# A recurrent layer step on one core: branch sums and weight splits given to VectorE, more row tiles of the out projection begun early, one mask product in place of two

## The chip, the cores and the metric

The kernel runs on one core of a Trainium2 chip. The metric is the device time of one execution in microseconds. The engines are named as in the profile: PE (TensorE; PEld is its weight load), DVE (VectorE, `V` in the code), ACT (ScalarE, `S`), POOL (GpSimd, `G`), and SP, whose queue issues most of the loads. Each engine works through its own list of instructions in order. Waits between engines go by semaphores.

## The reference

One inference step of a decoder layer with three token mixers side by side, for 512 prompt tokens and 8 x 4 sample tokens:

```python
h = rmsnorm(x, L['norm_pre_mix'])
proj = jnp.einsum('bsd,dc->bsc', h, L['w_in'])
xa, ga, bq, bf, bi, bg, cblk, gts = _split(proj, IN_SPLIT)
yA, nconv, nlru = rglru_branch(xa, ga, conv0, lru0, pos, ...)      # branch 0, width 512
yB, nhg = hgrn2_branch(bq, bf, bi, bg, hg0, lb, ...)               # branch 1, width 512
yC, nrw, nsh = rwkv7_branch(cblk, sh0, rw0, ...)                   # branch 2, width 512
br = jnp.stack([yA, yB, yC], axis=2)
up = jnp.einsum('bsnw,nwd->bsnd', br, L['w_branch'])
gates = jax.nn.sigmoid(gts.reshape(B, S, N_BRANCH, D_MODEL))       # D_MODEL = 1024
mix = jnp.einsum('bsd,de->bse', jnp.sum(gates * up, axis=2), L['w_out'])
x = x + rmsnorm(mix, L['norm_post_mix'])
h = rmsnorm(x, L['norm_pre_ffn'])
ff = (jax.nn.silu(h @ L['w_ffn_gate']) * (h @ L['w_ffn_up'])) @ L['w_ffn_down']
x = x + rmsnorm(ff, L['norm_post_ffn'])
x = x + rmsnorm((p @ L['w_ple']) * jax.nn.sigmoid(x @ L['w_ple_gate']), L['norm_ple'])
```

The change touches the sum over the three branches of gate times product, the product with `w_out` behind it, and, inside `rwkv7_branch`, the state update of the sample tokens: `st = st * wt - sk * (kkt * at) + vt * kt` for each of 8 sequences.

## The kernel before, in words

The 544 tokens are the columns of every tile, features are on the 128 partitions, so a tensor of width 1024 is 8 row tiles of 128x544 (`KD = 8`). A product of one row tile goes in two halves of 272 columns. Each fp32 operand is split in two parts, `hi` (a copy rounded to the format of the matmuls) and `lo` (what is left), and a product is hi·hi + hi·lo + lo·hi: three matmuls for each 128x128 block and half of the columns. Activations are split once (`act_h`, `act_l`). Weights are streamed: SP loads a row tile's weight into one of three buffers `raw`, ACT copies it to `hi` (L325) and a second engine subtracts to get `lo` (L326), half a tile (128x512) at a time. Which engine subtracts is read from a list `split_eng` with an entry for the first and one for the second half; a weight of the branches has only one half. The list holds `[V, V]` at first, `[G, G]` from the end of the RWKV part to the end of branch 2 and the gates of branch 1, and then `[V, V]` again. Three pairs of `hi` and `lo` halves are in flight. The weights of the first seven row tiles of `w_out` are kept (`held_weights`); their splits carry the names `ar<-raw` (`hi`) and `ar<-raw,ar` (`lo`), always on VectorE.

A branch (`branch`, L1487 on) goes over eight row tiles. For each, `th` is the gate (its tanh), `ps` the product of the branch with its weight (24 matmuls into a `pa` tile of two buffers), L1505 makes (th + 1) * ps on VectorE, and L1507 adds that to the row of the mix on GpSimd; the first branch writes the mix directly. The order of the branches is 0, 2, 1. The gates of branches 0 and 2 were computed earlier and put in DRAM (`gates`), from where SP loads them (L1501, `th<-gates`) into a work tile with two buffers; those of branch 1 stay on the chip.

Beside branch 2 runs the second half of HGRN2 (`hgrn_half(1)`), with raised priority: a scan by levels in which VectorE steps (L1302, L1305, L1306), small products on PE (`pb` tiles, four buffers) and masked copies out of them (L1328, L1317) follow each other, up to a last step L1355.

Behind branch 1, L1564 (ACT) and L1565 (VectorE) make `act_h` and `act_l` from each row of the mix, and the out projection runs by `by_halves`: first the prompt's first 272 columns of all row tiles, then `between_mix`, then the second half of the kept ones. Its first `ahead_of` row tiles (2) do all input rows but the last, then the last row of each of them, then each result is emptied: L1597 (a copy by ACT out of the `pb` tile) and L448 (its square). Each further row tile goes in one piece. `x` is loaded again for the residual (L168).

The update of the RWKV state for the sample tokens (`rw_decode`) goes by two pairs of heads in each of two calls. For a pair it spreads a 64x64 operand over the 8 sequences and masks it, for each of the two heads of the pair into 512 of the 1024 columns of `vm` (L993), and two matmuls follow.

No order is written out by hand: the code issues instructions in the order of the program with priorities (`high_priority`), and a scheduler with a timeline of its own sets, when the kernel is built, the order of each engine's list and of SP's loads. A change of an engine can thus move instructions elsewhere.

Of the kernel before, what the change touches and what calls it, by code (L numbers as in the profile page):

```python
# [12 lines left out]
ALU = mybir.AluOpType  # L13
# [4 lines left out]
NB = 8  # L18
# [4 lines left out]
KD = DM // P  # L23
# [8 lines left out]
NKEEP = 7  # L32
# [26 lines left out]
def kernel(  # L59
# [164 lines left out]
    smask = const.tile([64, NB], F32, name="smask")  # L224
# [703 lines left out]
    def rw_decode(y):  # L928

        v4, O4 = y.l4(y.v), y.l4(y.O)  # L930
        for m in range(2):
# [57 lines left out]
            V.tensor_tensor(O4[:, 2 * m:2 * m + 2, 256:288], ps[:, 0:2 * ND].rearrange("p (l n) -> p l n", l=2),  # L989
                            xo[:, :, 1, :], ALU.add)  # L990
            for i, l in enumerate(ls):
                for hp in range(2):
                    V.tensor_tensor(vm[0:64, 512 * hp:512 * hp + 512].rearrange("p (b n) -> p b n", b=NB),  # L993
                                    VUd[:, 2 * i + hp, :].unsqueeze(1).to_broadcast([64, NB, 64]),
                                    smask.unsqueeze(2).to_broadcast([64, NB, 64]), ALU.mult)
                ps = pb()
                with together():
                    for hp in range(2):
                        mm(ps[par[hp], :], KBtd[:, i, 64 * hp:64 * hp + 64], vm[0:64, 512 * hp:512 * hp + 512])
                sv = S0v[:, i]  # L1000
                V.tensor_tensor(sv, ps.rearrange("p (b n) -> p b n", b=NB), sv, ALU.add)
                V.tensor_tensor(sv, sv, y.PC[:, l, 4:12].unsqueeze(2).to_broadcast([P, NB, 64]), ALU.mult)
                G.dma_start(rws_out[:, l], sv)
# [209 lines left out]
    def hgrn_qvg(g):  # L1213

        q, v, gg = (alloc([P, 2, T], True) for _ in range(3))

        def silu2(dst, ct):
            ps = w_in_proj(ct)
            th = work.tile([P, T], F32, tag="ht", name=nm("th"))
            S.activation(half(th), ps[:, :, 0:272], AF.Tanh, scale=0.5)  # L1220
            V.scalar_tensor_tensor(half(dst), half(th), 1.0, ps[:, :, 0:272], op0=ALU.add, op1=ALU.mult)

        for l in range(2):
            silu2(j2(q)[:, l, :], BQ + 2 * g + l)
        for l in range(2):
            ps = w_in_proj(BI + 2 * g + l)
            S.activation(half(j2(v)[:, l, :]), ps[:, :, 0:272], AF.Copy)
        for l in range(2):
            silu2(j2(gg)[:, l, :], BG + 2 * g + l)
        return q, v, gg  # L1230
# [259 lines left out]
    def branch(n, yh, yl):  # L1490
        first = not mix
        if first:
            mix.append(gates[n] if n in gates else Rows(KD))
        m = mix[0]
        for j in range(KD):
            if n in gates:
                th = gates[n](j)
            else:
                th = work.tile([P, T], F32, tag="ht", name=nm("th"))
                if n in far:  # L1500
                    nc.sync.dma_start(th, far[n][:, j, :])  # L1501
                else:
                    gate(n, j, th)
            ps = proj(w_br[KD * n + j], 4, (yh, yl))
            V.scalar_tensor_tensor(half(m(j) if first else th), half(th), 1.0, ps[:, :, 0:272], op0=ALU.add, op1=ALU.mult)  # L1505
            if not first:
                G.tensor_tensor(m(j), m(j), th, ALU.add)  # L1507
        if n in gates and not first:
            gates[n].drop()
        yh.drop()  # L1510
        yl.drop()
# [39 lines left out]
    with tc.high_priority(1000):  # L1551
        yB = [hgrn_half(0, *fk[0], *qvg[0])]
    qvg.append(hgrn_qvg(1))
    branch(2, *yC)
    early_gates(1)
    with tc.high_priority(1500):
        yB.append(hgrn_half(1, *fk[1], *qvg[1]))
# [72 lines left out]
            f()  # L1630
        norm_ffn(0)

    by_halves([(w_out[j], KD) for j in range(KD)], HS, act, NKEEP, out_evac, between_mix, V)
    mix_steps = after_mix(1) + [lambda: norm_ffn(1)]
    p_hl = layer_input()
    ple = Rows(4 * NPLE // 2)
# [313 lines left out]
```

## Time and profile before

| | |
|---|---|
| times of three runs | 1212.57, 1194.4, 1202.06 us (median 1202.06) |
| the profiled execution | 1201.44 us, span 1199.7 us, mean granted clock 0.985 |
| busy, of the span | PE 1155.8 us (96%), DVE 763.5 (64%), ACT 582.9 (49%), POOL 317.8 (26%) |
| costliest split group on DVE, L326 | 234 instructions, 175.1 us |
| the same on POOL, L326 | 39 instructions, 60.2 us |

A row of a table by stretches reads: from and to in us from the span's start, length, then the busy time (and the number of instructions) of PE, PEld, DVE, ACT and POOL, the granted clock of PE, the busy share of the DMA engines and GB/s. A row of a timeline reads: start, duration, engine, line, operation, output and inputs, tile size, number of instructions taken together, and in brackets the idle time of the engine before it with what ended it. A row of groups reads: line, engine, operation, output and inputs, shape, number, busy time in all, mean duration in ns, idle time before them and what ended it.

### The profile page before, as it was taken

How to read it: one execution, taken by the hardware profiler on the slowest of the kernel's cores; microseconds unless marked ns; L12 is line 12 of the kernel's file. 1: busy time of each engine (PE TensorE's matmuls, PEld its weight loads, DVE VectorE, ACT ScalarE, POOL GpSimd, SP SyncE). 2: the span in 40 equal slices, each digit the busy share in tenths (PEclk: the TensorE clock that was granted, in tenths of full speed). 3: DMA queues.
4: the chain of work that ended last, by engine and by line, in shares of the span. 5: the costliest groups of instructions: out<-in, count | busy, mean ns of one | idle time of the engine just before them, and what ended most of it. 6: DMA issues, size and time to landing. Idle time of an engine off the chain costs nothing.

```text
span 1199.7 us, 24284 instructions
## 1 busy us (share of the span) xinstructions
PE 1155.8 (96%) x10048; PEld 1098.7 (92%) x10048; DVE 763.5 (64%) x1240; ACT 582.9 (49%) x1033; POOL 317.8 (26%) x367
## 2 busy tenths in 40 slices
PE   7999999999999999999999999999999999999995
PEld 6889999899899789889899898999999999999995
DVE  6789864944534759678214658765874576475766
ACT  6776355544633434453242555444552354255763
POOL 7327034310200002435543215101330330121001
PEclk9999999999999999989999999999999999999998
DMA  5212312122252431134522503123322332334302
GB/s 178 79 54 89 91 56 78 50 74 90 63 177 63 152 98 54 53 92 134 181 62 80 185 22 104 36 71 106 99 82 84 89 103 74 96 116 134 89 19 75
DMA packets 37470, 108.91 MB, mean 91 GB/s; under 512 B 4464, under 2 KB 6544, under 8 KB 37360
## 3 DMA queue, kind: packets, MB, share of 16 engines
q1 hardware_dynamic: 33856, 95.69, 26.1%
q0 software_dynamic: 3504, 11.67, 2.8%
q8 instruction: 79, 1.29, 0.4%
q14 instruction: 31, 0.25, 0.1%
HBM read 96.98 MB, written 10.36 MB: 89 GB/s over the span
## 4 chain that ended last, share of the span: by engine, by line
PE 75%; DVE 13%; DMA 4%; issue 4%; ACT 3%; POOL 0%; SPq 0%; DVEq 0%; ACTq 0%; POOLq 0%
PE pa L129 47%; PE pb L129 20%; PE pb L127 4%; PE pa L127 3%; DVE lo L326 2%; DVE ar L1302 1%; ACT hi L325 1%; DMA raw<-in_w_out_dram 1%; DVE ar L326 1%; PE pb L133 1%; DMA raw<-in_w_dn_b_dram 1%; PE pn L129 1%; DVE ar L1305 1%; PE pl L129 1%; DMA th<-gates 1%
## 5 line engine op out<-in xcount | busy, mean ns | idle before, releaser
L325 ACT ACTIVATE hi<-raw 128x512 fp32r<-128x512 f32 (+1 forms) x273 | 166.1, 610 | 310.4 <-PE pa L129 251.0
L326 DVE TENSOR_TENSOR lo<-raw,hi 128x512 fp32r<-128x512 f32 (+1 forms) x234 | 175.1, 751 | 151.4 <-ACT hi L325 147.0
L129 PE MATMUL pa<-act_h,hi 128*128 128x272 f32 (+1 forms) x1136 | 250.4, 296 | 0.5 <-ACT ar L544 0.3
L129 PE MATMUL pa<-act_h,lo 128*128 128x272 f32 (+1 forms) x1136 | 248.4, 294 | 1.5 <-DVE lo L326 1.5
L129 PE MATMUL pa<-act_l,hi 128*128 128x272 f32 (+1 forms) x1136 | 249.4, 295 | 0.0
L129 PE MATMUL pa<-ar,hi 128*128 128x272 f32 x1312 | 234.3, 292 | 9.8 <-ACT ar L475 5.6
L129 PEld LDWEIGHTS pa<-ar,hi 128*128 128x128 f32 x1312 | 191.9, 189 | 16.7 <-issue 7.0
L129 PEld LDWEIGHTS pa<-act_h,hi 128*128 128x128 f32 x1136 | 185.3, 192 | 5.4 <-issue 2.6
L129 PEld LDWEIGHTS pa<-act_l,hi 128*128 128x128 f32 x1136 | 185.0, 192 | 5.5 <-issue 3.8
L129 PEld LDWEIGHTS pa<-act_h,lo 128*128 128x128 f32 x1136 | 184.9, 192 | 5.3 <-issue 2.1
L129 PE MATMUL pa<-ar,lo 128*128 128x272 f32 x656 | 142.5, 291 | 0.0
L129 PE MATMUL pb<-act_h,ar 128*128 128x272 f32 x608 | 118.0, 290 | 3.9 <-ACT ar L448 1.9
L129 PEld LDWEIGHTS pa<-ar,lo 128*128 128x128 f32 x656 | 105.0, 190 | 2.2 <-issue 1.8
L129 PEld LDWEIGHTS pb<-act_h,ar 128*128 128x128 f32 x608 | 95.9, 188 | 5.6 <-ACT ar L448 2.1
L129 PE MATMUL pb<-ar,ar 64*64 64x64 f32 (+10 forms) x1496 | 91.4, 237 | 2.8 <-DVE st L905 1.6
L326 POOL TENSOR_TENSOR lo<-raw,hi 128x512 fp32r<-128x512 f32 x39 | 60.2, 1550 | 116.6 <-ACT hi L325 116.6
L129 PE MATMUL pb<-act_l,ar 128*128 128x272 f32 x304 | 88.1, 291 | 0.9 <-DVE act_l L1612 0.5
L129 PEld LDWEIGHTS pb<-ar,ar 64*64 64x64 f32 (+5 forms) x1496 | 75.5, 143 | 11.8 <-issue 4.2
L1718 POOL TENSOR_TENSOR ar<-raw,raw 128x512 f32<-128x512 f32 x10 | 14.6, 1456 | 202.6 <-DMA raw<-in_w_up_dram 202.6
L129 PEld LDWEIGHTS pb<-act_l,ar 128*128 128x128 f32 x304 | 57.2, 189 | 2.1 <-DVE act_l L1612 0.9
L326 DVE TENSOR_TENSOR lo<-ar,hi 128x512 fp32r<-128x512 f32 x40 | 34.5, 862 | 23.1 <-ACT hi L325 22.9
L422 DVE TENSOR_TENSOR ar<-ar,ar 128x544 fp32r<-128x544 f32 (+4 forms) x43 | 34.9, 818 | 12.9 <-ACT ar L421 11.2
(401 smaller groups left out, 1946.5 us busy)
## 6 DMA issues: line engine op xcount, KB each, us to landing
raw<-in_w_in_dram SPq DMA_DIRECT2D x61, 512.0 KB, 3.6
raw<-in_w_gate_dram SPq DMA_DIRECT2D x22, 512.0 KB, 3.6
raw<-in_w_up_dram SPq DMA_DIRECT2D x22, 512.0 KB, 3.6
raw<-in_w_dn_a_dram SPq DMA_DIRECT2D x24, 384.0 KB, 3.0
raw<-in_w_br_dram SPq DMA_DIRECT2D x24, 256.0 KB, 2.7
ar<-in_x_dram SPq DMA_DIRECT2D x16, 272.0 KB, 5.2
gates<-th POOLq DMA_DIRECT2D x16, 272.0 KB, 2.4
th<-gates SPq DMA_DIRECT2D x16, 272.0 KB, 2.9
```

The source lines that it names most:

```text
L127: PE.matmul(out, lhsT=lhsT, rhs=rhs, start=start, stop=stop, skip_group_check=True)
L129: PE.matmul(out, lhsT=lhsT, rhs=rhs, start=start, stop=stop)
L133: PE.transpose(out, in_, ident)
L325: S.activation(hi, raw, AF.Copy)
L326: eng.tensor_tensor(lo, raw, hi.bitcast(F32), ALU.subtract)
L422: V.tensor_tensor(lo, src, hi.bitcast(F32), ALU.subtract)
L1302: V.tensor_tensor(dv, bv, bv[:, :, :, hB - 1:hB].to_broadcast([P, 2, n // B, B]), ALU.subtract)
L1305: V.tensor_tensor(dv[:, :, :, 0:hB], dv[:, :, :, 0:hB], kv[:, :, :, 0:hB], ALU.mult)
L1718: G.tensor_tensor(q[0], a11, a21, ALU.subtract)
```

## The change

Four edits. The two mask products of a pair of heads become one instruction over 1024 columns (8 in all become 4). The sum of a branch into the mix goes from GpSimd to VectorE (16 instructions, for branches 2 and 1). The list `split_eng` is `[V, V]` for branch 2, so that its eight `lo` splits go from GpSimd to VectorE, and `[G, G]` again behind it. The out projection does all input rows but the last for four row tiles instead of two. Behind the first edit the line numbers are lower by one, and from the third on higher by one (L1564 becomes L1565, L1597 becomes L1598).

```diff
--- before.py
+++ after.py
@@ -989,10 +989,9 @@
             V.tensor_tensor(O4[:, 2 * m:2 * m + 2, 256:288], ps[:, 0:2 * ND].rearrange("p (l n) -> p l n", l=2),
                             xo[:, :, 1, :], ALU.add)
             for i, l in enumerate(ls):
-                for hp in range(2):
-                    V.tensor_tensor(vm[0:64, 512 * hp:512 * hp + 512].rearrange("p (b n) -> p b n", b=NB),
-                                    VUd[:, 2 * i + hp, :].unsqueeze(1).to_broadcast([64, NB, 64]),
-                                    smask.unsqueeze(2).to_broadcast([64, NB, 64]), ALU.mult)
+                V.tensor_tensor(vm[0:64, 0:1024].rearrange("p (h b n) -> p h b n", h=2, b=NB),
+                                VUd[:, 2 * i:2 * i + 2, :].unsqueeze(2).to_broadcast([64, 2, NB, 64]),
+                                smask.unsqueeze(1).unsqueeze(3).to_broadcast([64, 2, NB, 64]), ALU.mult)
                 ps = pb()
                 with together():
                     for hp in range(2):
@@ -1504,7 +1503,7 @@
             ps = proj(w_br[KD * n + j], 4, (yh, yl))
             V.scalar_tensor_tensor(half(m(j) if first else th), half(th), 1.0, ps[:, :, 0:272], op0=ALU.add, op1=ALU.mult)
             if not first:
-                G.tensor_tensor(m(j), m(j), th, ALU.add)
+                V.tensor_tensor(m(j), m(j), th, ALU.add)
         if n in gates and not first:
             gates[n].drop()
         yh.drop()
@@ -1551,7 +1550,9 @@
     with tc.high_priority(1000):
         yB = [hgrn_half(0, *fk[0], *qvg[0])]
     qvg.append(hgrn_qvg(1))
+    split_eng[:] = [V, V]
     branch(2, *yC)
+    split_eng[:] = [G, G]
     early_gates(1)
     with tc.high_priority(1500):
         yB.append(hgrn_half(1, *fk[1], *qvg[1]))
@@ -1630,7 +1631,7 @@
             f()
         norm_ffn(0)
 
-    by_halves([(w_out[j], KD) for j in range(KD)], HS, act, NKEEP, out_evac, between_mix, V)
+    by_halves([(w_out[j], KD) for j in range(KD)], HS, act, NKEEP, out_evac, between_mix, V, ahead_of=4)
     mix_steps = after_mix(1) + [lambda: norm_ffn(1)]
     p_hl = layer_input()
     ple = Rows(4 * NPLE // 2)
```

The order of every engine is the same as before up to the first of the updates of the RWKV sample state, and again from the fifth row tile of the out projection on. Between them it differs at three places.

**Branch 2 beside the second HGRN half.** VectorE's list before, around the fifth level of the scan; `th` with its number is the gate of one row tile of branch 2, `pa` its product, and L1505 makes gate times product:

```order
L1505 SCALAR_TENSOR_TENSOR th_6181<-th_6181,pa_6183 128x544
L1305 TENSOR_TENSOR ar_7001<-ar_7001,ar_4392 128x2x8x32
L1306 TENSOR_TENSOR ar_7001<-ar_7001,ar_5810 128x2x8x32
L1505 SCALAR_TENSOR_TENSOR th_6216<-th_6216,pa_6218 128x544
L1328 COPY_PREDICATED ar_6982<-lmask,pb_7111 64x8x2x16 x2
L1302 TENSOR_TENSOR ar_7000<-ar_6951 128x2x512
L1317 COPY ar_6982<-pb_7135 32x8x32
L1305 TENSOR_TENSOR ar_7000<-ar_7000,ar_4392 128x2x4x64
L1306 TENSOR_TENSOR ar_7000<-ar_7000,ar_5810 128x2x4x64
L1505 SCALAR_TENSOR_TENSOR th_6251<-th_6251,pa_6253 128x544
```

VectorE's list after, in the same place (all lines but L326 are one lower or, for the sum, L1506; `ar_4527` is a row of the mix; `lo_6288<-raw_6285,hi_6287` is a weight's split):

```order
L1504 SCALAR_TENSOR_TENSOR th_6177<-th_6177,pa_6179 128x544
L1305 TENSOR_TENSOR ar_6996<-ar_6996,ar_5806 128x2x16x16
L326 TENSOR_TENSOR lo_6288<-raw_6285,hi_6287 128x512
L1304 TENSOR_TENSOR ar_6997<-ar_6997,ar_4392 128x2x8x32
L1305 TENSOR_TENSOR ar_6997<-ar_6997,ar_5806 128x2x8x32
L1506 TENSOR_TENSOR ar_4527<-ar_4527,th_6177 128x544
L1504 SCALAR_TENSOR_TENSOR th_6212<-th_6212,pa_6214 128x544
L326 TENSOR_TENSOR lo_6323<-raw_6320,hi_6322 128x512
L1506 TENSOR_TENSOR ar_4527<-ar_4527,th_6212 128x544
L1327 COPY_PREDICATED ar_6978<-lmask,pb_7107 64x8x2x16 x2
L1301 TENSOR_TENSOR ar_6996<-ar_6947 128x2x512
L1504 SCALAR_TENSOR_TENSOR th_6247<-th_6247,pa_6249 128x544
```

Splits and sums of branch 2 now stand between the steps of the scan, and the copy out of the fifth level's product (`pb_7111`, now `pb_7107`) comes after two splits and two sums that were not in the list.

PE's list before, around the matmuls of the fifth level (`pb_7111`), in branch 2:

```order
L129 MATMUL pa_6218<-ar_5432,hi_6221 128x272 x2
L129 MATMUL pa_6218<-ar_5434,hi_6221 128x272 x2
L129 MATMUL pa_6218<-ar_5432,lo_6222 128x272 x2
L129 MATMUL pb_7111<-ar_7000 64x32 x16
L129 MATMUL pa_6253<-ar_5431,hi_6256 128x272 x2
L129 MATMUL pa_6253<-ar_5433,hi_6256 128x272 x2
L129 MATMUL pa_6253<-ar_5431,lo_6257 128x272 x2
```

PE's list after (the same product is `pb_7107`; `pa_6249` is the row that was `pa_6253`):

```order
L129 MATMUL pa_6249<-ar_5428,hi_6252 128x272 x2
L129 MATMUL pa_6249<-ar_5430,hi_6252 128x272 x2
L129 MATMUL pa_6249<-ar_5428,lo_6253 128x272 x2
L129 MATMUL pa_6249<-ar_5428,hi_6252 128x272 x2
L129 MATMUL pb_7107<-ar_6996 64x32 x16
L129 MATMUL pb_7131<-ar_6997 32x32 x8
L129 MATMUL pa_6249<-ar_5430,hi_6252 128x272 x2
```

The fifth level stood right before a row of the branch (`pa_6253`), and now stands in that row's last third: 57 instead of 41 branch matmuls lie between the fourth level's product and it.

**The loads of branch 2's gates.** SP's list before; a `raw` of `in_w_in` is a weight of the gates of branch 1, `in_x` the reload of x:

```order
L1501 DMA th_6286<-gates_3522 128x544
L168 DMA ar_7590<-in_x_dram 128x544 x2
L168 DMA ar_7591<-in_x_dram 128x544
L1501 DMA th_6321<-gates_3522 128x544
L168 DMA ar_7591<-in_x_dram 128x544
L330 DMA raw_6466<-in_w_in_dram 128x1024
L168 DMA ar_7592<-in_x_dram 128x544 x2
L330 DMA raw_6526<-in_w_in_dram 128x1024
L1501 DMA th_6356<-gates_3522 128x544
```

SP's list after, from the same row's gate (`th_6286`, now `th_6282`) on:

```order
L1500 DMA th_6282<-gates_3522 128x544
L330 DMA raw_6462<-in_w_in_dram 128x1024
L1500 DMA th_6317<-gates_3522 128x544
L168 DMA ar_7586<-in_x_dram 128x544 x2
L330 DMA raw_6522<-in_w_in_dram 128x1024
L168 DMA ar_7587<-in_x_dram 128x544 x2
L1500 DMA th_6352<-gates_3522 128x544
```

The two weights have moved up by some places, and four loads of x stand between the fourth gate load and the sixth, where six stood.

**The begin of the out projection.** ACT's list before; L1564 makes a row of `act_h`, and L325 are the `hi` halves of the row tiles of `w_out`: `raw_7683` is the third, `raw_7718` the fourth and `raw_7754`, `raw_7789`, `raw_7825`, `raw_7858` the fifth to the eighth:

```order
L1564 ACTIVATE act_h<-ar_4529 128x544
L325 ACTIVATE ar_7681<-raw_7683 128x512 x2
L1564 ACTIVATE act_h<-ar_4529 128x544
L1564 ACTIVATE act_h<-ar_4530 128x544
L325 ACTIVATE ar_7752<-raw_7754 128x512 x2
L325 ACTIVATE ar_7787<-raw_7789 128x512 x2
L325 ACTIVATE ar_7716<-raw_7718 128x512 x2
L1564 ACTIVATE act_h<-ar_4530 128x544
L325 ACTIVATE ar_7823<-raw_7825 128x512 x2
L325 ACTIVATE hi_7860<-raw_7858 128x512
```

ACT's list after (L1565 makes `act_h`; `raw_7669` is the third, `raw_7699` the fourth, `raw_7750`, `raw_7785`, `raw_7821` and `raw_7854` the fifth to the eighth):

```order
L1565 ACTIVATE act_h<-ar_4529 128x544
L325 ACTIVATE ar_7667<-raw_7669 128x512 x2
L1565 ACTIVATE act_h<-ar_4529 128x544
L325 ACTIVATE ar_7748<-raw_7750 128x512 x2
L1565 ACTIVATE act_h<-ar_4530 128x544
L325 ACTIVATE ar_7783<-raw_7785 128x512 x2
L325 ACTIVATE ar_7697<-raw_7699 128x512 x2
L1565 ACTIVATE act_h<-ar_4530 128x544
L325 ACTIVATE ar_7819<-raw_7821 128x512 x2
L325 ACTIVATE hi_7856<-raw_7854 128x512
```

The fifth row tile's halves have moved ahead of a row of the mix, and only two pairs, not three, stand between ACT's last two rows of the mix.

PE's list after, at the last input row of the four row tiles (`pb_7615`, `pb_7645`, `pb_7675`, `pb_7705`) and the begin of the fifth (`pb_7756`):

```order
L129 MATMUL pb_7615<-act_l,ar_7607 128x272
L129 MATMUL pb_7615<-act_h,ar_7608 128x272
L129 MATMUL pb_7645<-act_l,ar_7637 128x272
L129 MATMUL pb_7645<-act_h,ar_7638 128x272
L129 MATMUL pb_7675<-act_l,ar_7667 128x272
L129 MATMUL pb_7675<-act_h,ar_7668 128x272
L129 MATMUL pb_7705<-act_l,ar_7697 128x272
L129 MATMUL pb_7705<-act_h,ar_7698 128x272
L129 MATMUL pb_7756<-act_h,ar_7748 128x272
```

Before, the last matmul of the first row tile (`pb_7619<-act_h,ar_7612`) was followed by 17 matmuls, of the second to the fourth row tile, ahead of the fifth's first; now by 6.

## The prediction

> **What bounds the kernel now.** The page comes first. Its busy line says that TensorE works nearly all the time:
>
> ```profile
> PE 1155.8 (96%) x10048; PEld 1098.7 (92%) x10048; DVE 763.5 (64%) x1240; ACT 582.9 (49%) x1033; POOL 317.8 (26%) x367
> ```
>
> So the span is the sum of PE's work and of the moments in which PE waits, and a change that touches no matmul can only win such moments. The order of instructions is the same before and after up to the first decode update and again from the fifth row tile of the out projection on; the stage table (stretch, its length, then busy time of PE, PEld, DVE, ACT, POOL, then granted clock) cuts out what lies between:
>
> ```profile
> 383.00:432.00 49.00, 47.59 (x413) 40.22 (x412) 35.90 (x56) 17.92 (x30) 1.93 (x4) 1.00 0.40 126
> 432.00:545.00 113.00, 109.04 (x1003) 97.68 (x1002) 84.68 (x123) 56.31 (x91) 36.52 (x27) 0.97 0.24 72
> 545.00:590.00 45.00, 42.21 (x452) 39.08 (x451) 24.47 (x37) 13.26 (x25) 28.41 (x22) 1.00 0.55 173
> 590.00:644.00 54.00, 54.00 (x384) 51.55 (x383) 9.69 (x14) 20.10 (x29) 20.64 (x16) 0.94 0.26 80
> 644.00:684.00 40.00, 37.81 (x295) 36.80 (x294) 30.89 (x39) 19.32 (x36) 13.64 (x8) 1.00 0.47 150
> ```
>
> They are: branch 0 with the first decode update; projections beside the rest of RWKV and the first HGRN half; branch 2 beside the second HGRN half; the gates of branch 1; branch 1 and the start of the out projection. PE idles 1.41, 3.96, 2.79, 0.00 and 2.19 us in them: 10.35 us is all that the change can win from waits. The timeline of PE names the largest:
>
> ```profile
> 414.05 0.74 PE L129 MATMUL pa<-ar,hi 128*128 128x272 f32 x4 [1.41 <-DVE ar L1505]
> 526.75 1.16 PE L129 MATMUL pb<-ar,ar 128*128 128x128 f32 x8 [1.12 <-DVE ar L1284]
> 534.61 1.61 PE L129 MATMUL pb<-ar 128*64 128x32 f32 x40 [1.21 <-DVE ar L1284]
> 556.60 0.69 PE L129 MATMUL pb<-ar 128*32 128x32 f32 x16 [0.41 <-DVE ar L1306]
> 576.63 0.62 PE L129 MATMUL pa<-ar,hi 128*128 128x272 f32 x3 [1.71 <-DVE th L1505]
> 683.60 0.39 PE L129 MATMUL pb<-act_h,ar 128*128 128x272 f32 x1 [1.86 <-ACT ar L448]
> ```
>
> Two of them, at 576.63 and 683.60, end in what the change moves.
>
> **Branch 2: sums and splits to VectorE.** What GpSimd does there and what VectorE pays beside it (groups of 545 to 592, shapes apart), and what the same VectorE work takes undisturbed:
>
> ```profile
> L326 POOL TENSOR_TENSOR lo<-raw,hi 128x512 fp32r<-128x512 f32 x10 | 16.1, 1614 | 9.1 <-ACT hi L325 9.1
> L1507 POOL TENSOR_TENSOR ar<-ar,th 128x544 f32<-128x544 f32 x8 | 12.2, 1525 | 8.1 <-DVE th L1505 8.1
> L1302 DVE TENSOR_TENSOR ar<-ar 128x1024 f32<-128x1024 f32 x3 | 4.5, 1507 | 0.1
> L1306 DVE TENSOR_TENSOR ar<-ar,ar 128x512 f32<-128x512 f32 x4 | 3.9, 971 | 0.0
> L1305 DVE TENSOR_TENSOR ar<-ar,ar 128x512 f32<-128x512 f32 x3 | 3.2, 1054 | 0.3 <-ACT ar L1303 0.3
> L1505 DVE SCALAR_TENSOR_TENSOR th<-th,pa 128x544 f32<-128x544 f32 x8 | 5.7, 718 | 12.8 <-DMA th<-gates 9.6 <-POOL ar L1507 3.1
> ...
> 533.24 0.71 DVE L1306 TENSOR_TENSOR ar<-ar,ar 128x544 f32<-128x544 f32 x1
> 538.77 1.21 DVE L1302 TENSOR_TENSOR ar<-ar 128x1024 f32<-128x1024 f32 x1
> 543.88 0.67 DVE L1305 TENSOR_TENSOR ar<-ar,ar 128x512 f32<-128x512 f32 x1
> 648.06 0.69 DVE L326 TENSOR_TENSOR lo<-raw,hi 128x512 fp32r<-128x512 f32 x1
> ```
>
> A sum is a two-input add of 128x544, the shape of the 0.71 row; a split's second half is the 0.69 row. VectorE takes on 8 x 0.71 + 8 x 0.69 = 11.2 us. In turn it sheds what it lost beside GpSimd: 3 x (1.507 - 1.21) + 4 x (0.971 - 0.67) + 3 x (1.054 - 0.67) = 3.2 us. The stretch has 45.0 - 24.5 = 20.5 us of VectorE idle, so the net 8.0 us fits as a total. Where it falls matters: the three scan groups wait 0.1, 0.3 and 0.0 us in all, so beside them VectorE has no idle to speak of; its idle lies at the L1505 row, which waits 12.8.
>
> What the wait at 576.63 is made of, from the chain, VectorE and GpSimd:
>
> ```profile
> 567.64 1.36 POOL L1507 TENSOR_TENSOR ar<-ar,th 128x544 f32<-128x544 f32 x1
> 569.03 0.33 SPq L1501 DMA_DIRECT2D th<-gates  x1
> 569.03 6.61 DMA th<-gates
> 575.76 0.72 DVE L1505 SCALAR_TENSOR_TENSOR th<-th,pa 128x544 f32<-128x544 f32 x1 [6.04 <-DMA th<-gates]
> ```
>
> Two buffers hold `th`, so the gate load of a row may only be issued when the sum of two rows earlier has read its buffer: the sum ends at 569.00 and the load goes out at 569.03. It takes 6.61 us, beside loads of x and of input weights. On GpSimd a sum lasts 1.5 us on the mean and queues behind a split; on VectorE 0.71. I take 1.3 us of the 1.71 as won: about 0.65 by the shorter add, about 0.65 because a GpSimd split of 1.6 us no longer stands ahead in some of the cases. The ends: the whole 1.71, if the load no longer matters; nothing, if the load takes 6.61 us and a full two-row period or more has passed anyway. The order of SP says little either way: between the fourth gate load and the sixth stand two input weights and four x rows now, and two input weights and six x rows before.
>
> The scan chain of the second HGRN half shares VectorE. Seven splits and four sums now stand ahead of its L1355, 7 x 0.69 + 4 x 0.71 = 7.7 us, less 3.2: 4.5 us later. PE's order moves with it: the products of the fifth level stand 16 branch matmuls further back after the fourth's. A row of 24 of them takes 3.04 us:
>
> ```profile
> 651.23 1.78 POOL L1507 TENSOR_TENSOR ar<-ar,ar 128x544 f32<-128x544 f32 x1 [1.27 <-DVE ar L1505]
> 654.27 1.77 POOL L1507 TENSOR_TENSOR ar<-ar,ar 128x544 f32<-128x544 f32 x1 [1.26 <-DVE ar L1505]
> ```
>
> so 16 give 2.0 us there. That part of the delay PE fills with branch work; for the rest I take zero, as the wait for the chain at 556.60 is only 0.41 us long, and bound it by 4.5 - 2.0 = 2.5 lost and by those 0.41 won. The end of the half is covered: its output is wanted by branch 1 at 644, and PE has gate projections without a pause from 590 to 644 (the 54.00 of 54.00). If that cover were gone, each us of delay would cost one.
>
> **Branch 1: sums to VectorE.** Groups of 644 to 676:
>
> ```profile
> L1507 POOL TENSOR_TENSOR ar<-ar,ar 128x544 f32<-128x544 f32 x8 | 13.6, 1710 | 23.0 <-DVE ar L1505 23.0
> ...
> L1565 DVE SCALAR_TENSOR_TENSOR act_l<-ar,act_h 128x544 fp32r<-128x544 f32 x7 | 7.8, 1110 | 1.3 <-ACT act_h L1564 1.3
> L326 DVE TENSOR_TENSOR lo<-raw,hi 128x512 fp32r<-128x512 f32 x6 | 7.6, 1267 | 2.3 <-ACT hi L325 2.3
> ```
>
> VectorE gains 8 x 0.71 = 5.7 us and sheds 7 x (1.11 - 0.71) + 6 x (1.267 - 0.69) = 6.3 us: nothing net. What goes is latency, 1.71 - 0.71 = 1.0 us from each branch product to its row of the out projection's input.
>
> **Out projection.** The wait at 683.60 read backwards:
>
> ```profile
> 672.55 0.66 ACT L1564 ACTIVATE act_h<-ar 128x544 fp32r<-128x544 f32 x1 [3.61 <-POOL ar L1507]
> 674.33 3.69 DVE L326 TENSOR_TENSOR ar<-raw,ar 128x512 fp32r<-128x512 f32 x6
> 676.85 4.34 DMA raw<-in_w_out_dram
> 681.22 1.67 ACT L325 ACTIVATE hi<-raw 128x512 fp32r<-128x512 f32 x3 [0.96 <-DMA raw<-in_w_out_dram]
> 682.79 0.47 ACT L1597 ACTIVATE ar<-pb,vec 128x272 f32<-128x272 f32 x1
> ```
>
> PE fills four banks and needs the first one emptied; ACT empties it only at 682.79, since the splits of the eighth tile stand ahead in its order, and those wait for a load that left at 676.85, when the sixth tile's splits (second pair of the six) were done. They began at 674.33 because ACT had sat until 672.55 on a sum. After the change two pairs of splits come between ACT's last two waits for sums. I estimate: VectorE's last branch product at about 670.1, 3.04 us a row after the products that the two L1507 rows waited for, the sixth tile's splits done by 674.5 instead of 676.8, the load out and home 2.3 us earlier, ACT free for the first bank at about 680.5. PE would be through its four banks at about 680.3 and go on at about 681.5: 2.1 us won. Ends: 0, if raw buffers come free no earlier, and 2.9, the whole wait and 1.0 of latency. With four tiles held to the last input row, only 6 matmuls (0.76 us) now follow the first tile's last one, where 17 (2.15 us) did, so a part of the wait that emptying takes (from 682.79 to PE's 683.60, 0.8 us) will remain.
>
> **Decode mask.** Eight products become four of double length:
>
> ```profile
> L993 DVE TENSOR_TENSOR ar<-ar,smask 64x512 f32<-64x512 f32 x8 | 5.3, 679 | 2.3 <-PE pb L129 1.3 <-ACT ar L983 1.0
> ```
>
> 4 x 1.21 (the 128x1024 row) against 5.3 us: 0.5 us of VectorE less, the first of each pair 0.5 us later. PE has branch 0 matmuls beside it; I take 0. With two spread operands in one pattern it may cost more than 1.21; at twice that, 4.8 us of VectorE, it would lengthen the wait at 414.05 by 1.2 at most per update pair.
>
> **Sum**, against the profiled execution's 1201.44 us (span 1199.7; the median of the runs shown is 1202.06, 0.6 above it): 1201.44 - 1.3 - 2.1 = **1198.0**.
>
> **The rivals.** (1) *The loads keep both waits.* The gate load still takes 6.6 us, and the eighth weight still arrives when it did: 1201.4. For it: both waits end in a transfer. Against: each transfer is released by a sum or by what sits behind one.
>
> (2) *VectorE becomes the bound in branch 2*, the slower case. GpSimd's splits waited 9.1 us for ACT in that stretch (row above), in an order in which nothing else stood behind them. On VectorE the steps L1305 and L1306 stand behind, and behind these PE's products and the emptying of the branch banks. It decides from where a split waits longer than the 2.0 us by which PE's order was stretched: the 4.5 us of delay with 3 to 4 us of such waits cost PE about 6 us at 550 to 575; with the 2.1 us won later: 1201.44 + 6 - 2.1 = 1205.3. Against: the new order puts splits where ACT has delivered, if the loads come on time. The Trainium skill, "Perfetto Trace Analysis", section "Optimizing Scalar/DVE Operations", says that with a saturated DVE it may pay to offload to Scalar or even GPSIMD; by that the move goes the wrong way here, and this rival would be the forecast.
>
> (3) *The clock shifts.* Three stretches ran at half clock:
>
> ```profile
> 510.00:515.00 5.00, 5.00 (x30) 4.96 (x30) 3.08 (x4) 2.39 (x5) 0.87 (x2) 0.72 0.91 256
> 537.00:541.00 4.00, 4.00 (x26) 3.87 (x25) 3.92 (x7) 0.93 (x2) 0.97 (x1) 0.61 0.26 70
> 595.00:602.00 7.00, 7.00 (x32) 6.87 (x33) 1.48 (x2) 2.48 (x4) 1.64 (x2) 0.53 0.35 141
> ```
>
> They cost 0.28 x 5 + 0.39 x 4 + 0.47 x 7 = 6.3 us, and each follows small HGRN products that the change shifts against the projections. Losing the last, 3.3 us: 1194.7; gaining one of 1.6: 1199.6. The Trainium skill, "TensorE: Matmul & The Clock Gate", section "What's actually happening", ties the half clock to an idle window of some 3.4 us; by that no wait here, 1.86 at most, would cause one, and this rival would have no chance. The rows differ: PE counts as busy throughout all three.
>
> **How the numbers follow.** Forecast 0.50 (1195.5 to 1200.5); rival 1 0.20; rival 2 0.15; rival 3 0.15, mostly downward. The runs shown lie 7.7 below and 10.5 above their median, so the range reaches from 1190 (forecast less that 7.7) to 1209 (forecast and that 10.5, which takes in rival 2). A measurement of this kernel tells about 2% (24 us) from no change. All waits and half-clock stretches of the touched part together are 10.35 + 6.3 = 16.7 us, so faster by 2% has 0.02, slower 0.03, for a jam that I don't see, and 0.95 lies between.
>
> **What would show it.** Right: PE's wait before branch 2's sixth row under 0.6 us, VectorE's waits for gate loads well under the 9.6 us that they total now, no VectorE split above 1 us in branch 1, the out projection's fifth tile after a wait of about 1.2 us. Rival 1: these two waits as long as now. Rival 2: PE waiting on L1305, L1306 or L1505 for over 3 us between 545 and 580. Rival 3: other stretches of half clock. The forecast fails if scheduling puts a late weight in front of the scan chain, or if run-to-run spread exceeds the change.

## The result, and the profile after

The changed kernel takes 1190.95 us (median of 20 runs, 1185.24 to 1199.59) against 1201.66 us (20 runs, 1194.3 to 1212.57) for the kernel before: a ratio of 0.9926, with a 95% interval of 0.9905 to 0.9948. That is no change by the 2% line, a gain by the interval, and inside the range given, at its lower end. The forecast of 3.4 us won was too small by a factor of three, and 1190.95 lies below the 1195.5 to 1200.5 to which the prediction gave its main chance.

The profiled execution took 1199.59 us (span 1197.9), 8.6 above the median, at a mean clock of 0.977, where the one of before had 0.985. Both kernels' times follow the clock from run to run, so it has to be taken out before two spans are compared. The stretch table of the trace after, in two stretches that ran at half clock:

```profile
234.00:254.00 20.00, 20.00 (x83) 17.59 (x82) 14.47 (x21) 1.26 (x2) 5.49 (x4) 0.50 0.04 15
374.00:380.00 6.00, 6.00 (x60) 5.97 (x57) 0.00 (x0) 0.31 (x2) 0.00 (x0) 0.50 0.09 33
```

The same 20 us of the trace before:

```profile
234.00:254.00 20.00, 18.79 (x125) 17.10 (x126) 16.84 (x29) 3.36 (x7) 7.37 (x7) 0.91 0.17 59
```

These 20 us lie ahead of everything that the change touches; PE starts 83 matmuls in them where it started 125. At this place the traces of `mask` and `tied` (below) have 20.5 us of half clock as well, and all three have a mean clock of 0.977; the other eleven have 3.4 us there. Over all runs of this study, with each kernel's own mean taken out, 0.001 of clock goes with 0.93 us. Below, "at the same clock" is a time moved along this line to 0.985: 1191.9 us for the changed kernel and 1201.5 for the one before (82 runs), a gain of **9.7 us, give or take 0.7** (here and below twice the standard error).

Where it comes from shows in PE's rows of the trace after. Its busy line:

```profile
PE 1158.3 (97%) x10048; PEld 1105.5 (92%) x10048; DVE 772.0 (64%) x1260; ACT 584.3 (49%) x1033; POOL 277.2 (23%) x343
```

and the five stages of the prediction, with ends that follow the work (stretch, length, then PE, PEld, DVE, ACT, POOL, granted clock):

```profile
383.00:437.00 54.00, 53.06 (x481) 47.41 (x480) 37.30 (x56) 20.30 (x34) 1.62 (x3) 1.00 0.39 122
437.00:547.00 110.00, 106.94 (x982) 97.25 (x981) 84.35 (x123) 57.33 (x90) 33.75 (x25) 0.94 0.23 72
547.00:590.00 43.00, 42.90 (x466) 40.46 (x464) 32.43 (x54) 13.72 (x25) 7.11 (x7) 1.00 0.56 186
590.00:643.00 53.00, 53.00 (x385) 50.59 (x384) 9.63 (x14) 20.07 (x29) 20.11 (x16) 0.97 0.26 80
643.00:681.00 38.00, 37.07 (x297) 36.85 (x295) 29.86 (x47) 19.09 (x35) 0.00 (x0) 1.00 0.54 160
```

PE idles 0.94, 3.06, 0.10, 0.00 and 0.93 us, 5.0 in all where it idled 10.35. Branch 2 has lost all but 0.1 of its 2.79 us. What is left, in PE's timeline:

```profile
419.64 0.61 PE L129 MATMUL pa<-ar,hi 128*128 128x272 f32 x3 [0.94 <-DVE ar L1504]
486.79 0.69 PE L129 MATMUL pb<-ar 128*32 128x32 f32 x16 [0.55 <-DVE ar L1305]
529.66 0.49 PE L129 MATMUL pb<-ar,ar 128*128 128x128 f32 x2 [0.36 <-DVE ar L1283]
537.76 0.45 PE L129 MATMUL pb<-ar 128*64 128x32 f32 x6 [2.16 <-DVE ar L1283]
680.95 0.39 PE L129 MATMUL pb<-act_h,ar 128*128 128x272 f32 x1 [0.93 <-ACT ar L448]
```

That accounts for some 5 of the 9.7 us. The 5 is rough, because the waits of a trace change with its clock. PE's list in `ahead4` (below) is that of the kernel before up to the out projection: from PE's 3601st to its 5951st matmul the trace of before has 8.2 us of waits, 13.7 us of half clock and a length of 273.9 us, that of `ahead4` 10.8 us of waits, no half clock and 270.7 us.

The rest is not in any wait: PE's work itself became shorter. The matmuls that use the masked operand of `rw_decode`, as a group of the trace before:

```profile
L129 PE MATMUL pb<-ar,ar 64*64 64x512 f32 x16 | 8.5, 612 | 0.0
```

and its first pair in PE's timeline:

```profile
390.50 1.05 PE L129 MATMUL pb<-ar,ar 64*64 64x512 f32 x2
392.05 1.07 PE L129 MATMUL pb<-ar,ar 64*64 64x512 f32 x2
```

The same group of the trace after:

```profile
L129 PE MATMUL pb<-ar,ar 64*64 64x512 f32 x16 | 4.3, 615 | 0.0
```

and its first pair:

```profile
399.02 1.08 PE L129 MATMUL pb<-ar,ar 64*64 64x512 f32 x4
```

Each of the eight matmuls has two records. One record lasts as long as before (612 and 615 ns), but the group covers half the time. Before, the two matmuls of a pair stood apart in PE's list (1.55 us from start to start in this one), with other matmuls in between. This is the order made when the kernel is built, in which each matmul had a mask product of its own ahead of it; in the execution PE waited for neither (0.0 in the group row). After, both have the one product ahead of them, stand next to each other, and the four records take the 1.08 us of two. So the lists differ here too, a place that is not among the three named with the change. Each uses 64 rows and 64 columns of the array (`64*64`) and they write different halves of the partitions. This is 4.2 us, as large a part of the gain as any. The Trainium skill, "TensorEngine Tiling (Array Packing)", section "Key Properties", says that different tiles of the array can execute in parallel; these rows agree, and add that it takes neighbours in PE's list.

On VectorE and GpSimd the prediction's reading holds. Groups of 545 to 592, after:

```profile
L1304 DVE TENSOR_TENSOR ar<-ar,ar 128x512 f32<-128x512 f32 x5 | 3.4, 677 | 0.0
L1305 DVE TENSOR_TENSOR ar<-ar,ar 128x512 f32<-128x512 f32 x5 | 3.4, 677 | 0.0
L326 DVE TENSOR_TENSOR lo<-raw,hi 128x512 fp32r<-128x512 f32 x8 | 5.4, 679 | 0.3 <-ACT hi L325 0.3
L1506 DVE TENSOR_TENSOR ar<-ar,th 128x544 f32<-128x544 f32 x8 | 6.1, 762 | 0.1
L1504 DVE SCALAR_TENSOR_TENSOR th<-th,pa 128x544 f32<-128x544 f32 x8 | 5.7, 716 | 4.6 <-DMA th<-gates 4.5
```

The scan steps are back at 0.68 us from 0.97 and 1.05, the splits wait 0.3 us for ACT where GpSimd's waited 9.1, and VectorE waits 4.5 us for gates where it waited 9.6.

### The profile page after: what moved, and what is told of

It is laid out like the page before. It is cut to its first block, busy times and chain, and to the rows that moved or that the text cites. A ratio compares the mean times of both kernels' runs of the same rounds, so it can differ in the third digit from the quotient of the medians.

```text
span 1197.9 us, 24267 instructions
## 1 busy us (share of the span) xinstructions
PE 1158.3 (97%) x10048; PEld 1105.5 (92%) x10048; DVE 772.0 (64%) x1260; ACT 584.3 (49%) x1033; POOL 277.2 (23%) x343
## 4 chain that ended last, share of the span: by engine, by line
PE 80%; DVE 11%; issue 3%; DMA 3%; ACT 3%; POOL 0%; SPq 0%; DVEq 0%; ACTq 0%; POOLq 0%
PE pa L129 51%; PE pb L129 21%; PE pb L127 4%; PE pa L127 3%; DVE lo L326 2%; ACT hi L325 1%; PE pb L133 1%; DVE ar L326 1%; DMA raw<-in_w_dn_b_dram 1%; PE pn L129 1%; PE pl L129 1%; DVE ar L1608 0%; DVE ar L1301 0%; DVE act_l L1613 0%; DMA ar<-in_x_dram 0%
## 5 line engine op out<-in xcount | busy, mean ns | idle before, releaser
L325 ACT ACTIVATE hi<-raw 128x512 fp32r<-128x512 f32 (+1 forms) x273 | 166.1, 611 | 322.7 <-PE pa L129 273.6
L326 DVE TENSOR_TENSOR lo<-raw,hi 128x512 fp32r<-128x512 f32 (+1 forms) x242 | 179.8, 746 | 157.9 <-ACT hi L325 156.0
L129 PEld LDWEIGHTS pb<-ar,ar 64*64 64x64 f32 (+5 forms) x1496 | 79.5, 148 | 12.5 <-issue 4.6
L326 POOL TENSOR_TENSOR lo<-raw,hi 128x512 fp32r<-128x512 f32 x31 | 46.5, 1501 | 144.5 <-ACT hi L325 140.3
L326 DVE TENSOR_TENSOR lo<-ar,hi 128x512 fp32r<-128x512 f32 x40 | 34.8, 870 | 22.1 <-ACT hi L325 22.0
```

Of the source, the lines that this page charges most:

```text
L129: PE.matmul(out, lhsT=lhsT, rhs=rhs, start=start, stop=stop)
L325: S.activation(hi, raw, AF.Copy)
L326: eng.tensor_tensor(lo, raw, hi.bitcast(F32), ALU.subtract)
```

## The experiments

All are told against the kernel before. The runs below the first came in three groups (`mask` to `no_mask`, `sums` to `ahead4`, `no_ahead` to `qvg_v`), on three chips, each with its own runs of the kernel before beside it (35, 35 and 12), to which the ratios refer; at the same clock those three sets agree within 0.5 us, and the last column uses all 82:

| run | median us (runs) | ratio, 95% interval | us won at the same clock |
|---|---|---|---|
| the whole change | 1190.95 (20) | 0.9926, 0.9905 to 0.9948 | 9.7 ± 0.7 |
| `mask` | 1195.84 (12) | 0.9950, 0.9919 to 0.9980 | 4.3 ± 1.2 |
| `mask_apart` | 1208.12 (12) | 1.0046, 1.0021 to 1.0071 | -5.2 ± 1.0 |
| `tied` | 1201.02 (12) | 0.9994, 0.9961 to 1.0027 | 0.4 ± 1.2 |
| `no_mask` | 1191.59 (12) | 0.9926, 0.9896 to 0.9956 | 5.9 ± 1.0 |
| `sums` | 1193.97 (12) | 0.9952, 0.9930 to 0.9973 | 4.3 ± 0.8 |
| `splits` | 1198.18 (12) | 0.9992, 0.9960 to 1.0025 | 1.2 ± 1.1 |
| `sums_splits` | 1193.81 (12) | 0.9943, 0.9913 to 0.9973 | 5.0 ± 1.1 |
| `ahead4` | 1198.37 (12) | 0.9994, 0.9975 to 1.0014 | 0.2 ± 1.0 |
| `no_ahead` | 1188.92 (6) | 0.9915, 0.9881 to 0.9949 | 9.4 ± 1.0 |
| `no_sums` | 1191.24 (7) | 0.9925, 0.9898 to 0.9953 | 8.1 ± 1.5 |
| `no_splits` | 1191.40 (6) | 0.9924, 0.9897 to 0.9952 | 8.3 ± 1.4 |
| `qvg_v` | 1185.84 (6) | 0.9880, 0.9851 to 0.9908 | 12.6 ± 1.1 |

The last column assumes that the clock is chance and not the kernel's doing; mean clocks ran from 0.984 to 0.989. That holds for the long stretch at 234 us, but not wholly behind 383 us, where stretches of half clock also follow PE's own waits (last section). Where the two columns disagree (`no_mask`: mean clock 0.988), both are given weight below.

**The mask alone.** The edit is the first hunk of the change.

> The kernel before with only the merged mask product. Side-by-side theory: with one mask for both heads the two 64x512 matmuls of a pair become ready together, stand next to each other in PE's list and run beside one another on two 64x64 parts of the array: the trace after shows starts 0.007 us apart, where the trace before shows the second pass 0.46 us behind and 0.98 us for each matmul alone. Four pairs then save 4 x 0.98 = 3.9 us of PE time, and the time falls by 3 to 5 us (ratio about 0.9967). Waits theory (all of the gain is from PE's waits in branch 2 and the out projection): ratio 1.000 within 0.001.

Measured: 4.3 us at the same clock, as side by side foretells, and a ratio that excludes 1. The group row of this kernel is that of the change:

```profile
L129 PE MATMUL pb<-ar,ar 64*64 64x512 f32 x16 | 4.3, 614 | 0.0
```

and PE's waits in branch 2 and the out projection are still in its timeline:

```profile
579.65 0.61 PE L129 MATMUL pa<-ar,hi 128*128 128x272 f32 x3 [1.44 <-DVE th L1504]
...
685.12 0.39 PE L129 MATMUL pb<-act_h,ar 128*128 128x272 f32 x1 [2.07 <-ACT ar L448]
```

This kernel's PE list, too, differs from that of before in some 600 places, and its trace has 9.1 us of waits where before had 10.4, so a part of the 4.3 may be the new order's.

**The mask merged, the matmuls apart.** Behind the merged product:

```diff
+                V.tensor_copy(vm[0:64, 512:513], vm[0:64, 512:513])
```

> The kernel before with the merged mask, and behind it a copy of one column (column 512) onto itself on VectorE, for which only the second matmul of a pair waits, so that the two are apart in PE's list again. Side-by-side theory: each matmul takes 0.98 us by itself again, the gain of the merged mask is gone, ratio 1.000 within 0.002. If the gain of the merged mask came from VectorE's shorter work (about 0.5 us less in all), it would stay: ratio as in the run with the merged mask alone.

Measured: the gain is gone, and 5.2 us more, outside the 0.002 that was expected; a shorter VectorE list was not what won. The pairs are apart again in the group:

```profile
L129 PE MATMUL pb<-ar,ar 64*64 64x512 f32 x16 | 8.6, 614 | 0.0
```

and the loss beyond zero sits in longer waits of PE, 16.0 us in all in its trace from 383 us to the fifth row tile where before had 10.4. PE's list differs from that of before in some 900 places: the order moved with the small copy. The longest of the waits:

```profile
472.02 0.31 PE L129 MATMUL pb<-ar 128*32 128x32 f32 x4 [1.85 <-DVE ar L1284]
...
497.81 0.66 PE L129 MATMUL pb<-ar 128*64 128x64 f32 x4 [2.44 <-DVE ar L1306]
...
560.53 0.66 PE L129 MATMUL pb<-ar 128*64 128x32 f32 x16 [1.50 <-DVE ar L1306]
```

**Two masks, the matmuls tied.** The two mask products of before, and behind them:

```diff
+                V.tensor_copy(vm[0:64, 511:513], vm[0:64, 511:513])
```

> The kernel before with its two mask products for each pair, and behind them a copy of two columns (511 and 512) onto themselves on VectorE, for which both matmuls of a pair wait, so that they are next to each other in PE's list without the merge. VectorE has more work than before. Side-by-side theory: 3 to 4 us won as with the merged mask, ratio about 0.997, starts of a pair 0.007 us apart. Theory that the shorter VectorE work counts: no gain or a small loss, ratio 1.000 to 1.001.

Measured: 0.4 ± 1.2 us, a miss of the 3 to 4. The pairs do run side by side, and the group shows the 4.2 us won:

```profile
L129 PE MATMUL pb<-ar,ar 64*64 64x512 f32 x16 | 4.3, 614 | 0.0
```

but the new order pays it back in waits, 17.8 us in all over the same work. PE's timeline of before has one of 1.41 us for the first of these lines, at 414.05, and none over 1 us from there to 520:

```profile
423.02 0.52 PE L129 MATMUL pa<-act_h,hi 128*128 128x272 f32 x2 [2.47 <-DVE ar L1506]
...
498.06 0.63 PE L129 MATMUL pb<-ar 128*32 128x32 f32 x15 [1.16 <-DVE ar L1307]
...
500.59 0.64 PE L129 MATMUL pb<-ar 128*32 128x32 f32 x8 [1.87 <-DVE ar L1318]
...
502.99 0.76 PE L129 MATMUL pb<-ar 128*64 128x64 f32 x5 [1.33 <-DVE ar L1307]
```

The fair partner of this run is `mask_apart`, which has the same kind of small copy: from PE's 4627th matmul on, in 498 us, the two lists are the same by the names in the profile, and `tied` is 5.6 ± 1.5 us faster, though it gives VectorE more work and PE idles longer in its trace. So the mechanism is shown by the group rows of `mask`, `mask_apart` and `tied`, and its worth in time by `mask` and by these two against each other; against the kernel before, neighbours alone won nothing that can be told.

**All but the mask.** The changed kernel with the first hunk undone.

> The changed kernel with the two separate mask products put back (sums and splits on VectorE, four row tiles held, kept). Side-by-side theory: the gain of 9 us is cut by 3.9, ratio to the kernel before 0.9955 to 0.997; PE's wait before branch 2's sixth row stays away and the one at the fifth row tile of the out projection stays about 0.9 us. Waits theory: ratio as of the whole change, 0.9926.

Measured: the ratio is that of the whole change, which the waits theory foretold; its runs had a mean clock of 0.988. At the same clock 5.9 us are left, which with the mask's 4.3 makes 10.2 against 9.7. The group stands at 8.5 us again:

```profile
L129 PE MATMUL pb<-ar,ar 64*64 64x512 f32 x16 | 8.5, 612 | 0.0
```

By the ratio alone this run would not decide; the group row and `mask` do. Part of its higher clock may be its own: the 2.16 us wait of the changed kernel at 537.76, which ends in 6.8 us of half clock there, is 1.21 us in this order and no half clock follows it.

**The sums alone.** The `V.tensor_tensor(m(j), m(j), th, ALU.add)` of the third place of the diff.

> The kernel before with only the sums of branches 2 and 1 on VectorE. Buffer theory of the prediction: the sum ends about 1 us earlier, so the gate loads go out earlier and ACT gets each row of the mix about 1 us sooner: PE's wait before branch 2's sixth row (1.71 us before) falls to about 1 us, and the one at the fifth row tile of the out projection (1.86) to about 1 us; 1.5 to 2.5 us in all at the same clock. Rival: both stay, since each ends in a load, 0.

Measured: 4.3 us, twice the expectation. The wait before the sixth row is gone altogether, and the out projection's is 0.70 of 1.86; one scan wait has grown from 0.46 (PE's timeline):

```profile
552.41 0.78 PE L129 MATMUL pb<-ar 128*64 128x32 f32 x20 [1.36 <-DVE ar L1306]
...
676.05 0.39 PE L129 MATMUL pb<-act_h,ar 128*128 128x272 f32 x1 [0.70 <-ACT ar L448]
```

**The splits alone.**

```diff
+    split_eng[:] = [V, V]
     branch(2, *yC)
+    split_eng[:] = [G, G]
```

> The kernel before with only branch 2's weight splits on VectorE, sums left on GpSimd. Buffer theory: a sum no longer queues behind a split on GpSimd, so the wait before the sixth row falls by about 0.7 us; the out projection's wait stays at 1.86. Contention theory: VectorE's two-input operations of the scan chain keep running 0.3 to 0.4 us longer beside the sums left on GpSimd, so the chain waits (0.46, 0.41 and 0.22 us at 553 to 561) stay or grow, and the gain is under 1 us or a loss up to 2.

Measured: 1.2 ± 1.1 us. Branch 2's wait falls from 1.71 to 0.44, and now ends in ACT, while the out projection keeps its own: either edit is enough for branch 2, and the contention theory's growing scan waits did not come. PE's timeline:

```profile
572.30 0.74 PE L129 MATMUL pa<-ar,hi 128*128 128x272 f32 x4 [0.44 <-ACT hi L325]
...
676.66 0.39 PE L129 MATMUL pb<-act_h,ar 128*128 128x272 f32 x1 [1.75 <-ACT ar L448]
```

**Sums and splits.** Both edits, nothing else.

> The kernel before with sums and branch 2's splits on VectorE, GpSimd idle in branch 2; separate masks, two row tiles held. If the two edits only work together (GpSimd silent, VectorE's scan steps at 0.68 us as in the trace after, where they took 0.97 to 1.05), branch 2 has no wait of PE above 0.3 us and the gain is more than the sum of the two single runs: 4 to 5 us at the same clock. If they add up: the sum of the two single runs within 1 us.

Measured: 5.0 ± 1.1 us. That fits the sum, 4.3 + 1.2, and as well the sums alone: beside them the splits' share is 0.7 ± 1.3. More than the sum it is not. PE's wait before the sixth row is just above the 0.3 us expected, and that of the out projection is 1.00 (PE's timeline):

```profile
574.59 0.61 PE L129 MATMUL pa<-ar,hi 128*128 128x272 f32 x3 [0.35 <-DVE th L1505]
...
675.64 0.39 PE L129 MATMUL pb<-act_h,ar 128*128 128x272 f32 x1 [1.00 <-ACT ar L448]
```

**Four row tiles held, alone.** The last hunk.

> The kernel before with only four row tiles of the out projection held to the last input row. The prediction's reading: what ACT waits for (sums on GpSimd) is unchanged, so the wait at the fifth row tile stays at 1.5 to 2.5 us (fewer matmuls cover the emptying), and nothing is won: 0 within 1 us. Rival: the early matmuls fill PE while the last rows of the mix arrive, and 1 us or more is won by this edit alone.

Measured: 0.2 ± 1.0 us. The wait got longer, 3.11 us, as the expectation's reading has it (fewer matmuls left to cover the emptying, ACT still waiting for GpSimd; not tested apart). PE's timeline:

```profile
678.55 0.40 PE L129 MATMUL pb<-act_h,ar 128*128 128x272 f32 x1 [3.11 <-ACT ar L448]
```

**The change without its fourth edit.**

> The changed kernel with two row tiles held again instead of four. If the fourth edit only pays once the sums are on VectorE (the two runs so far at the same clock: sums and splits 4.9 us won, with four tiles held as well 6.1), this loses 1 to 1.5 us of the 9.8 that the whole change wins at the same clock: 8.3 to 8.8 won, and PE's wait at the fifth row tile is about as long but later. If the fourth edit is worth nothing: 9.8.

Measured: 9.4 ± 1.0 us; its wait in PE's timeline is as long as with the edit. The fourth edit is worth nothing that these runs can tell.

```profile
670.90 0.39 PE L129 MATMUL pb<-act_h,ar 128*128 128x272 f32 x1 [0.89 <-ACT ar L448]
```

**The change without the sums.**

> The changed kernel with the sums on GpSimd again. The sums alone won 4.2 us at the same clock. If the parts add up, this is left with 9.8 - 4.2 = 5.6 us, and the wait at the fifth row tile is back at 2.5 us or more, since ACT waits for GpSimd's sums again. If the splits do the same work for branch 2 (their run alone had no wait above 0.5 us there), it is left with about 7.

Measured: 8.1 ± 1.5 us. The wait at the fifth row tile is back, but PE has no other above 0.3 us from 545 on, so that the splits do the sums' work in branch 2:

```profile
674.04 0.39 PE L129 MATMUL pb<-act_h,ar 128*128 128x272 f32 x1 [2.37 <-ACT ar L448]
```

Beside the splits the sums are worth 9.7 - 8.1 = 1.6 us by this run and 5.0 - 1.2 = 3.8 by `sums_splits`, each with some 1.6 of uncertainty: how much of the 4.3 the splits could replace stays open.

**The change without the splits.**

> The changed kernel with branch 2's splits on GpSimd again. The splits alone won 1.1 us at the same clock, and 0.7 beside the sums. Additive theory: 8.7 to 9.1 us left of 9.8. If GpSimd's silence beside the scan is what counts, 2 us or more are lost and waits for L1304 or L1305 come back at 550 to 562.

Measured: 8.3 ± 1.4 us, between the theories, which it does not separate; and two short scan waits are what came back in PE's timeline:

```profile
547.23 0.95 PE L129 MATMUL pb<-ar 128*64 128x32 f32 x26 [0.32 <-DVE ar L1305]
...
549.93 0.44 PE L129 MATMUL pb<-ar 128*32 128x32 f32 x8 [0.26 <-DVE ar L1305]
```

**More splits to VectorE.** The `[V, V]` moved ahead of the second HGRN half's inputs, with the whole change:

```diff
+    split_eng[:] = [V, V]
     qvg.append(hgrn_qvg(1))
-    split_eng[:] = [V, V]
     branch(2, *yC)
```

> The changed kernel with the weight splits of the second half of HGRN2's inputs (hgrn_qvg(1)) on VectorE too. In the trace after GpSimd's 12 splits at 437 to 547 take 1.78 us each, and VectorE's L1304 and L1305 beside them 0.98 and 0.85 us where they take 0.68 in branch 2. Contention theory: with GpSimd silent PE's waits for the scan chain there (0.55, 0.36 and 2.16 us) shrink by 1 to 2 us, and it is 1 to 2 us faster than the whole change. Load theory: VectorE is busy 84 of 110 us there and gets up to 8 us more, so the chain falls back and it is 1 to 3 us slower.

Measured: 1185.84 us, 12.6 us won, 2.9 ± 1.2 more than the change. The contention theory holds, with more than the 1 to 2 us it gave; GpSimd keeps 12.4 us of other work there, without the 21.4 us of splits. The groups of the 110 us ahead of branch 2, of the changed kernel:

```profile
L1304 DVE TENSOR_TENSOR ar<-ar,ar 128x512 f32<-128x512 f32 x6 | 5.9, 976 | 1.1 <-ACT ar L1302 1.1
L1305 DVE TENSOR_TENSOR ar<-ar,ar 128x512 f32<-128x512 f32 x6 | 5.1, 854 | 0.0
```

and of this one:

```profile
L1305 DVE TENSOR_TENSOR ar<-ar,ar 128x512 f32<-128x512 f32 x6 | 4.1, 677 | 0.0
L1304 DVE TENSOR_TENSOR ar<-ar,ar 128x512 f32<-128x512 f32 x6 | 4.1, 677 | 0.0
```

PE's timeline of this one:

```profile
546.33 0.89 PE L129 MATMUL pb<-ar 128*64 128x32 f32 x23 [0.93 <-DVE ar L1305]
```

This is the only wait of PE above 0.3 us between 411 and 667 in this kernel; the 0.55, 0.36 and 2.16 of the changed one are gone. This version beats both kernels.

## Why the prediction was right or wrong

**Sign and range: right; size: too small.** At the same clock 9.7 us went where 3.4 were forecast. That the range held the result is luck: its lower end, 1190, was the forecast less the spread between runs, and no step of the prediction led there.

**The bound: half right.** "A change that touches no matmul can only win such moments" held for waits. The step that failed is its use on this change: the mask does not alter a matmul, but it sets when its two matmuls become ready, and so whether they stand next to each other. The rows of the trace after show it (`x4` in place of two `x2`); the prediction did not look at PE's list there. Its table of the largest waits also left out two longer than the 0.41 that it lists, 0.90 us at 473.94 and 0.65 at 483.34; they are in its total of 10.35.

**Decode mask: wrong.** "I take 0" was 4.3 us in `mask` and 4.2 in the group row. VectorE's side was as forecast (1.21 us for the merged product); what was won lay on PE.

**Branch 2: right in mechanism, low in size.** 1.3 of 1.71 us was forecast; the whole wait went. The scan chain, taken as zero, also gave its waits at 553 to 561 (none above 0.1 us after). Whether VectorE's shorter steps or the products' later place in PE's list did this is not separated: `splits` alone has none of these waits, `sums` alone one of 1.36. The two of them in PE's timeline of before that the prediction did not show:

```profile
553.48 0.31 PE L129 MATMUL pb<-ar 128*64 128x32 f32 x4 [0.46 <-DVE ar L1306]
560.60 0.28 PE L129 MATMUL pb<-ar 128*32 128x32 f32 x3 [0.22 <-DVE ar L1317]
```

The two causes that were each given 0.65 us are not halves: `sums` and `splits` each take most of the wait away alone.

**Out projection: right.** PE goes on with the fifth tile at 680.95, with 0.93 us of wait. Its 6000th matmul, in branch 1, starts at 654.83 after and at 655.25 before, and from there to the fifth tile it takes 26.1 and 28.3 us: 2.2 us won against 2.1 forecast. The wait itself gives 0.93 of them; the rest lies ahead of it, among 200 matmuls in both traces. VectorE's splits in branch 1 are at 0.69 us from 1.27, as forecast. The cause is the sums (0.70 us of wait in `sums`, 1.75 in `splits`, 2.37 in `no_sums`); four held tiles add nothing in `ahead4` or beside the rest.

**Rival 1 (loads keep both waits): refuted**, both waits fell. **Rival 2 (VectorE becomes the bound): refuted**: VectorE's splits waited 0.3 us for ACT, and more work on VectorE won again in `qvg_v`. The Trainium skill's advice that spoke for it, "Perfetto Trace Analysis", section "Optimizing Scalar/DVE Operations", has a condition that was not met here, a saturated VectorE (it was busy 32.4 of 43 us in branch 2). The same paragraph of the Trainium skill adds that offloading between these two might not help, as they share a port; the traces agree in effect, since VectorE's 128x512 steps took 0.98 us beside GpSimd's splits and 0.68 without. **Rival 3 (the clock): not borne out as an effect of the change.** The kernel before has runs from 0.975 to 0.994, the changed one from 0.977 to 0.992, with means of 0.986 and 0.985. But waits are not ruled out as a cause of half clock, though the prediction reads PE as busy throughout its three stretches: the one at 537 to 541 begins 2.1 us after the wait of 1.21 us at 534.61 ended, and the last section has more of this kind.

## What to carry to other kernels

When PE is the bound, a VectorE edit is also to be priced on PE: look in the built order for small matmuls that become neighbours. Two of them on different parts of the array took 1.08 us together here, and 1.05 to 1.07 each when apart. Before work is kept on GpSimd, compare the same VectorE operation beside it and alone (0.98 against 0.68 us here); when VectorE has idle time in the stage, taking the work over can cost less than what the two engines cost each other. Where the clock varies from run to run, list it beside each time before a difference of a per cent is read. And do not add up the waits of a single trace as if they were its time: they change with the clock (8.2 and 10.8 us here for the same list).

## What the runs showed that was not expected

- Of 82 runs of the kernel before, 10 have a clock of 0.975 to 0.977 and take 1208.6 to 1213 us; the 12 with 0.990 or more take 1195.0 to 1199.2. Time and clock go together with a correlation of -0.94. The 17 us more of half clock at 234 us, in the three traces with 0.977, make 8.5 us by an estimate (half of 17), about this distance. What decides which run gets it stays open.
- PE kept running at half clock while it was busy all the time: 20.0 of 20.0 us at 234 to 254. The Trainium skill, "TensorE: Matmul & The Clock Gate", section "What's actually happening", ties the half clock to an idle window of some 3.4 us; no run here shows an idle window of that length ahead of such a stretch between 100 and 1100 us, but shorter waits often stand there. All 14 traces have a wait of 1.6 us right ahead of the stretch at 234. Between 383 and 700 us they have 33 stretches: 19 begin right behind 3.4 us in which PE idled 1.1 to 3.0 us, and 14, at 500 to 511 and at 582 to 599, behind 3.4 us without any idling. A wait of PE may thus cost more than its own length; no run here tests that by itself. The stretch table of `mask_apart` around its wait of 1.78 us shows it:

```profile
415.60:419.00 3.40, 1.62 (x13) 1.44 (x12) 3.34 (x5) 3.40 (x7) 0.00 (x0) 1.00 0.00 0
419.00:422.40 3.40, 3.40 (x17) 3.40 (x16) 3.34 (x6) 1.11 (x3) 0.00 (x0) 0.50 0.48 154
```

- A copy of one or two columns (`mask_apart`, `tied`) moved the order enough to cost 5.2 and some 4 us against what the pairs alone would give; a single edit's time in a scheduled kernel holds the accidents of its order.
